# A decoder layer's last FFN: gate and up by seven half products (Strassen) for nine of eleven pairs of tiles, with the sums of weights made ahead in DRAM

## The chip, the cores and the metric

One core of one Trainium2 chip (trn2). The metric is the device time of one execution in microseconds (us). Before the change the median is 1129.5 us over 3 runs, from 1129.4 to 1129.79.

## What is computed

One layer over 512 tokens of width 1024, all in fp32: half a SwiGLU FFN with 2816 hidden columns, two token mixers side by side with one output projection, cross attention to 256 memory tokens, the same FFN again with other weights, a final norm. The part that the change touches, cut from the reference:

```python
def swiglu(h, w_gate, w_up, w_down):
    return (jax.nn.silu(h @ w_gate) * (h @ w_up)) @ w_down
...
x = x + 0.5 * swiglu(rmsnorm(x, ffn2_norm), ffn2_w_gate, ffn2_w_up, ffn2_w_down)
return rmsnorm(x, final_norm)
```

## The kernel before

Everything is held transposed: `X[d]` (d from 0 to 7) is 128 of the 1024 columns by 512 tokens. A product of two fp32 matrices is three matmuls in fp32r (`mm3`, L124 to L129): each operand is split into a high part (a copy to fp32r, made by ScalarE, ACT) and a low part (source minus high, made by VectorE, DVE), and high x high, high x low and low x high are summed in PSUM. So no weight can be used before it was loaded by a DMA that SyncE (SP) issues, copied by ACT (`whi`, L103) and subtracted by DVE (`wlo`, L104). `load_weight` (L109 to L118) does this with three pools of three buffers: raw, hi and lo. A raw buffer is free again when DVE has subtracted, a hi or lo buffer when the last matmul that reads it has ended.

The stages, in order of the trace: the first FFN (to about 460 us), the mixers (to about 560 us), the output projection `w_out` and the cross attention (to about 748 us; its eight query weights `wq` are loaded from 621 us on), the second FFN (748 to 1115 us), the last norm. `ffn` works in two chunks of 11 hidden tiles of 128 columns. For each hidden tile, gate and up are 8 x 3 matmuls each of 128x128 by 512 tokens, from one 512 KB weight each. `evacuate` (L241 to L256) multiplies the two sums by the norm's factor `R`, applies SiLU, multiplies, and splits the hidden tile. Then the down product adds the chunk's 11 tiles to each of the eight `X[d]`. The last chunk's down runs in two halves of 256 tokens (L311 to L333), with the down weights of six of the eight d kept in SBUF for the second half (tiles `wk`).

What sets the order: the framework's scheduler places the instructions when the kernel is built, for each engine apart. At run time each engine, SP's queue included, works strictly in its own order: an instruction that waits holds all behind it. In the second FFN before the change, SP's queue is weights in the order in which the matmuls need them, gate, up, gate, up, and then the down weights of the chunk.

Of the kernel before, what the change touches and what calls it, by code (L numbers as in the profile page):

```python
# [17 lines left out]
F32 = mybir.dt.float32  # L18
# [22 lines left out]
SB = 6  # L41
LINE = 512

FILL = 56

# [9 lines left out]
def body(tc, I, out):  # L55
# [3 lines left out]
    with ctx:  # L59
# [4 lines left out]
        hp = ctx.enter_context(tc.tile_pool(name="hp", bufs=40))  # L64
        wp = ctx.enter_context(tc.tile_pool(name="wp", bufs=3))
# [43 lines left out]
        def load_weight(src, shape, cuts=1):  # L109
# [8 lines left out]
            return hi, lo  # L118

# [94 lines left out]
        def ffn(norm, gate, up, down, nxt, first=None, between=None):  # L214
            h = (norm.H, norm.L)
            with tc.tile_pool(name="ffn", bufs=2) as fp:
# [40 lines left out]
                for c in range(NCHUNK):  # L257
                    hid = ([], [])
                    for j in range(CF):
                        f = c * CF + j  # L260
                        ps = []
                        for src in (gate, up):
                            if f == 0 and src is gate and first is not None:
                                w = first()
                            else:
                                w = load_weight(src[f], [KD, P])
# [4 lines left out]
                            if first is not None and f == 1 and R is None:  # L271
                                R = factor()
                        pending.append(ps)
                        if first is not None and f == 0:
                            continue
                        if R is None:
                            R = factor()
                        while pending:
                            evacuate(pending.pop(0), hid)
                    if c < NCHUNK - 1 or nxt is not None:  # L280
                        for d in range(KD):
                            w = [load_weight(down[c, d, :, j0:j1, :], [j1 - j0, P])
                                 for j0, j1 in halves]
                            down_tile(d, w, hid, slice(0, S), halves)
                            if c == NCHUNK - 1:
                                nxt.add(d)
                            elif between is not None:
                                between(d)
# [3 lines left out]
                    thirds = ((0, 4), (4, 8), (8, CF))  # L292
                    kept = {}

                    def weights(d, keep):
                        if d in kept:
                            return kept[d], thirds
                        if not keep:
                            return [load_weight(down[c, d, :, j0:j1, :], [j1 - j0, P])
                                    for j0, j1 in halves], halves  # L300
                        kept[d] = []
                        for j0, j1 in thirds:
                            raw = wp.tile([P, j1 - j0, P], F32, name="wraw3", tag="wraw")
# [591 lines left out]
```

## Time and profile before

| what | value |
|---|---|
| median of 3 runs | 1129.5 us |
| the profiled execution | 1129.09 us; its span from first to last instruction 1127.3 us |
| mean granted clock of TensorE | 0.995 |
| busy: PE / DVE / ACT / POOL | 1110.1 / 590.9 / 425.0 / 74.3 us |
| second FFN's gate, up and first down (748 to 1050 us) | PE busy 301.52 of 302 us |
| second FFN's last down, two token halves (1050 to 1115 us) | PE busy 65.00 of 65 us |
| tail after it (1115 to 1127.3 us) | PE busy 2.26 us |

PE is TensorE's matmuls, PEld its weight loads, DVE is VectorE, ACT ScalarE, POOL GpSimd, SP SyncE, which issues DMAs. A row of the groups of instructions (by line, engine and form) gives line, engine, operation, output and input tiles with shape, count, then busy us and the mean ns of one, then the idle time before them. The waits view gives total us, times, longest. A windows row gives the stretch, its length, each engine's busy us with the count of instructions, and, at its end, the granted clock, the DMA share and GB/s. A timeline row begins with start and duration in us. A profiled matmul's duration is longer than the distance to the next, since matmuls overlap in the array; what counts is start to start.

### The profile page before, as it was taken

What the parts mean: (1) busy time and instruction counts of PE and PEld (TensorE: products, weight loads), DVE (VectorE), ACT (ScalarE), POOL (GpSimd) and SP (SyncE); (2) the same over time, 40 slices, a digit from 0 to 9 for tenths busy, and PEclk for the clock granted to TensorE, in tenths of its full rate; (3) what the DMA queues carried; (4) which work ended last, traced back from release to release, by engine and by line L of the source; (5) the groups of instructions that cost most, each with busy time, mean ns of one, the idle gap of its engine ahead of it and who ended that gap; (6) DMA issues with size and microseconds to landing.
All of it is one profiled execution on the core that took longest, in us unless ns stands there. A gap on an engine that the chain in (4) does not pass through costs nothing. (4 is left out here: it accounts for less than half of the span.)

```text
span 1127.3 us, 13958 instructions
## 1 busy us (share of the span) xinstructions
PE 1110.1 (98%) x5472; PEld 934.7 (83%) x5472; DVE 590.9 (52%) x1027; ACT 425.0 (38%) x672; POOL 74.3 (7%) x98
## 2 busy tenths in 40 slices
PE   9999999999999999999989999999999999999996
PEld 7788888888888888888868988878888888888996
DVE  4544533444444447679796555455444334445542
ACT  6333312233233434568665344333332222333421
POOL 2000100000002200011121000120000000000011
PEclk9999999999999999999999999999999999999998
DMA  6322334222233423110136421222222333223511
GB/s 220 113 94 89 115 89 126 105 94 94 72 92 109 149 90 108 38 48 29 57 118 203 147 75 57 72 97 90 98 93 66 103 113 111 95 94 115 155 64 38
DMA packets 39698, 110.79 MB, mean 98 GB/s; under 512 B 4432, under 2 KB 9296, under 8 KB 39632
## 3 DMA queue, kind: packets, MB, share of 16 engines
q1 hardware_dynamic: 39632, 109.89, 30.3%
q8 instruction: 43, 0.70, 0.2%
q14 instruction: 23, 0.19, 0.1%
HBM read 107.78 MB, written 2.10 MB: 97 GB/s over the span
## 5 line engine op out<-in xcount | busy, mean ns | idle before, releaser
L103 ACT ACTIVATE whi<-wraw 128x1024 fp32r<-128x1024 f32 (+2 forms) x213 | 202.8, 953 | 513.9 <-PE acc L128 298.6
L104 DVE TENSOR_TENSOR wlo<-wraw,whi 128x1024 fp32r<-128x1024 f32 (+2 forms) x213 | 237.0, 1115 | 163.0 <-ACT whi L103 162.7
L127 PE MATMUL acc<-hH,whi 128*128 128x512 f32 x768 | 301.0, 392 | 0.6 <-ACT hH L202 0.6
L128 PE MATMUL acc<-hL,whi 128*128 128x512 f32 x768 | 299.4, 390 | 0.8 <-DVE hL L203 0.8
L129 PE MATMUL acc<-hH,wlo 128*128 128x512 f32 x768 | 299.4, 390 | 0.5 <-DVE wlo L104 0.5
L128 PEld LDWEIGHTS acc<-hL,whi 128*128 128x128 f32 x768 | 144.3, 188 | 31.5 <-DVE hL L203 1.5
L127 PEld LDWEIGHTS acc<-hH,whi 128*128 128x128 f32 x768 | 144.3, 188 | 31.4 <-ACT hH L202 1.0
L129 PEld LDWEIGHTS acc<-hH,wlo 128*128 128x128 f32 x768 | 144.3, 188 | 30.7 <-DVE wlo L104 1.0
L127 PE MATMUL acc<-hidH,whi 128*128 128x512 f32 (+1 forms) x308 | 115.6, 375 | 0.0
L129 PE MATMUL acc<-hidH,wlo 128*128 128x512 f32 (+1 forms) x308 | 115.3, 374 | 0.0
L128 PE MATMUL acc<-hidL,whi 128*128 128x512 f32 (+1 forms) x308 | 115.3, 374 | 0.0
L170 POOL TENSOR_TENSOR sq<-sq 128x512 f32<-128x512 f32 (+1 forms) x39 | 49.2, 1260 | 775.5 <-ACT sq L178 775.1
L247 DVE TENSOR_TENSOR u<-acc,R 128x512 f32<-128x512 f32 x44 | 30.4, 690 | 121.6 <-PE acc L129 121.6
L243 DVE TENSOR_TENSOR gp<-acc,R 128x512 f32<-128x512 f32 x44 | 30.4, 691 | 85.4 <-PE acc L129 81.7
L129 PEld LDWEIGHTS acc<-hidH,wlo 128*128 128x128 f32 x308 | 58.1, 189 | 10.3
L128 PEld LDWEIGHTS acc<-hidL,whi 128*128 128x128 f32 x308 | 58.1, 188 | 10.3
L127 PEld LDWEIGHTS acc<-hidH,whi 128*128 128x128 f32 x308 | 58.1, 189 | 10.2
L127 PE MATMUL acc<-whi,hH 128*128 128x512 f32 x160 | 62.5, 391 | 0.0
L129 PE MATMUL acc<-whi,hL 128*128 128x512 f32 x160 | 62.4, 390 | 0.0
L230 DVE SCALAR_TENSOR_TENSOR x<-acc,x 128x512 f32<-128x512 f32 (+1 forms) x40 | 23.3, 584 | 74.6 <-PE acc L129 74.6
L128 PE MATMUL acc<-wlo,hH 128*128 128x512 f32 x160 | 62.3, 390 | 0.0
L178 ACT ACTIVATE sq<-x 128x512 f32<-128x512 f32 (+1 forms) x48 | 26.1, 551 | 41.5 <-DVE x L230 38.9
(213 smaller groups left out, 1488.1 us busy)
## 6 DMA issues: line engine op xcount, KB each, us to landing
wraw<-up SPq DMA_DIRECT2D x44, 512.0 KB, 3.5
wraw<-gate SPq DMA_DIRECT2D x43, 512.0 KB, 3.5
wraw<-down SPq DMA_DIRECT2D x28, 384.0 KB, 3.1
wraw<-w_in SPq DMA_DIRECT2D x20, 512.0 KB, 3.5
wraw<-down SPq DMA_DIRECT2D x28, 320.0 KB, 2.9
wraw<-w_out SPq DMA_DIRECT2D x16, 256.0 KB, 2.7
wraw<-wv SPq DMA_DIRECT2D x8, 512.0 KB, 3.5
wraw<-wk SPq DMA_DIRECT2D x8, 512.0 KB, 4.2
```

The source lines that it names most:

```text
L103: ins = nc.scalar.activation(hi, src, AF.Copy)
L104: nc.vector.tensor_sub(lo, src, f32(hi))
L127: nc.tensor.matmul(ps, lhsT=aH, rhs=bH, start=start, stop=False)
L128: nc.tensor.matmul(ps, lhsT=aH, rhs=bL, start=False, stop=False)
L129: nc.tensor.matmul(ps, lhsT=aL, rhs=bH, start=False, stop=stop)
L170: nc.gpsimd.tensor_add(self.parts[0], self.parts[0], sq)
L178: nc.scalar.activation(sq, src, AF.Square)
L230: nc.vector.scalar_tensor_tensor(X[d][:, tok], acc, 0.5, X[d][:, tok], op0=ALU.mult, op1=ALU.add)
L243: nc.vector.tensor_mul(gp, ps[0], R)
L247: nc.vector.tensor_mul(u, ps[1], R)
```

## The change

The second FFN becomes a function of its own, `ffn_last`. Its 22 hidden tiles are taken as 11 pairs. The first two pairs (`PLAIN`) are done as before. For each of the other nine, gate and up (s = 0 and 1) are done by Strassen's method in Winograd's form: the weight block of two tiles by 1024 rows is cut in four quarters (two tiles, two halves of the 8 k-blocks), the token operand in four (two halves of k, two halves of the tokens), and instead of eight quarter products seven are made, each of 4 x 3 matmuls of 128x128 by 256 tokens. They run in the order 1, 5, 6, 2, 7, 3, 4.

- Four of the seven need sums of weight quarters (products 5, 6, 7, 3). `sum_step` makes them in DRAM long before: four plain copies of 256 KB issued by SP, and four accumulating DMAs of 256 KB issued by GpSimd. There are 18 such sums, nine pairs times two; ten steps run in the first FFN, eight ahead of the query weights of the cross attention, and two more flush the last accumulations.
- The token operands of the products (`operands`, four times) are built from `X`, gain and `R` by DVE and split by ACT and DVE, between the plain tiles' work. `R` goes into them, so the evacuation of the nine pairs does not multiply by it.
- The weights of products 1, 6, 7, 4 use the three-buffer pools (gate and up in one 128x1024 tile); those of 5, 2 and 3 come as two 128x512 tiles each (`wq`, with halves `wqh`, `wql`) in the big pool `hp`, which also holds the hidden tiles.
- Products are combined by adding in PSUM and by copies (ACT, `p1`, `p5`, `v`, 128x256) and adds (DVE).
- The chunks are now 4, 6, 6 and 6 tiles instead of 11 and 11, so the down product runs three times over all 512 tokens, and once, for the last 6 tiles, in two halves of 256 tokens. All eight down weights are now kept for the second half.

```diff
+PLAIN = 2
+ORDER = (1, 5, 6, 2, 7, 3, 4)
+KH = KD // 2
...
+        sums, todo = {}, [(n, j) for j in range(PLAIN, NF // 2) for n in range(2)]
+        def sum_step():
+            m = len(sums)
+            def add(i, src, back):
+                if 0 <= m - back < len(todo):
+                    n, j = todo[m - back]
+                    a = (I["gate2"], I["up2"])[n]
+                    nc.gpsimd.dma_start(sums[n, j][i], src(a[2 * j], a[2 * j + 1], sums[n, j]),
+                                        accum_op=ALU.add)
+            if m < len(todo):
+                n, j = todo[m]
+                a = (I["gate2"], I["up2"])[n]
+                a1, a2 = a[2 * j], a[2 * j + 1]
+                t = dram.tile([P, 4, KH, P], F32, name=f"sums{n}_{j}")
+                sums[n, j] = {i: t[:, x] for x, i in enumerate((5, 6, 7, 3))}
+                with tc.issue_after(last["dma"].ins):
+                    for i, src in ((5, a2[:, :KH]), (7, a2[:, :KH]), (6, a1[:, :KH]),
+                                   (3, a1[:, KH:])):
+                        nc.sync.dma_start(sums[n, j][i], src)
+            else:
+                sums[None, m] = None
+            add(5, lambda a1, a2, s: a2[:, KH:], 0)
+            add(7, lambda a1, a2, s: a1[:, :KH], 0)
+            add(6, lambda a1, a2, s: s[5], 1)
+            add(3, lambda a1, a2, s: s[6], 2)
...
+                        each(f)
...
+        LO, HI = slice(0, S // 2), slice(S // 2, S)
+        def ffn_last(norm, gate, up, down, sums):
+            h = (norm.H, norm.L)
+            with tc.tile_pool(name="spad", bufs=1) as spad, \
+                    tc.tile_pool(name="sp", bufs=1) as sp, \
+                    tc.tile_pool(name="ffn", bufs=1) as fp:
+                nc.vector.memset(spad.tile([P, SHIFT], F32, name="spad")[:, 0:1], 0.0)
+                R = None
+                B11, B2 = ([], []), ([], [])
+                T13, T24 = ([], []), ([], [])
+                def operands(k):
+                    x = []
+                    for d in (k, k + KH):
+                        t = hp.tile([P, S], F32, name="xg", tag="h")
+                        nc.vector.scalar_tensor_tensor(t, X[d], gcol(norm.off, d), R,
+                                                       op0=ALU.mult, op1=ALU.mult)
+                        x.append(t)
+                    a, b = x
+                    t13 = hp.tile([P, S], F32, name="t13", tag="h")
+                    nc.vector.tensor_sub(t13[:, LO], a[:, LO], a[:, HI])
+                    nc.vector.tensor_sub(t13[:, HI], b[:, HI], a[:, HI])
+                    t24 = hp.tile([P, S], F32, name="t24", tag="h")
+                    nc.vector.scalar_tensor_tensor(t24[:, LO], b[:, HI], -1.0, t13[:, LO],
+                                                   op0=ALU.mult, op1=ALU.subtract)
+                    nc.vector.scalar_tensor_tensor(t24[:, HI], t24[:, LO], -1.0, b[:, LO],
+                                                   op0=ALU.mult, op1=ALU.subtract)
+                    for n, pair, src in (("b11", B11, a[:, LO]), ("b2", B2, b),
+                                         ("t13", T13, t13), ("t24", T24, t24)):
+                        for i, hl in enumerate("hl"):
+                            pair[i].append(sp.tile([P, src.shape[-1]], F32R, name=f"{n}{hl}{k}"))
+                        split(pair[0][k], pair[1][k], src)
...
+                def weights_of(i, j):
+                    raws = []
+                    for n, src in enumerate((gate, up)):
+                        raws.append({1: src[2 * j][:, :KH], 2: src[2 * j][:, KH:],
+                                     4: src[2 * j + 1][:, KH:]}.get(i) if i in (1, 2, 4)
+                                    else sums[n, j][i])
+                    if ORDER.index(i) % 2:
+                        w = []
+                        for src in raws:
+                            raw = hp.tile([P, KH, P], F32, name="wq", tag="h")
+                            last["dma"] = nc.sync.dma_start(raw, src)
+                            pair = tuple(hp.tile([P, KH, P], F32R, name=n, tag="h")
+                                         for n in ("wqh", "wql"))
+                            split(*pair, raw)
+                            w.append(pair)
+                        return w
+                    raw = wp.tile([P, 2, KH, P], F32, name="wraw", tag="wraw")
+                    hi = wp.tile([P, 2, KH, P], F32R, name="whi", tag="whi")
+                    lo = wp.tile([P, 2, KH, P], F32R, name="wlo", tag="wlo")
+                    for n, src in enumerate(raws):
+                        last["dma"] = nc.sync.dma_start(raw[:, n], src)
+                    split(hi, lo, raw)
+                    return [(hi[:, n], lo[:, n]) for n in range(2)]
+                def strassen(j, hid):
+                    right = {1: (B11, LO), 2: (B2, LO), 3: (B2, HI), 4: (T24, HI),
+                             5: (T13, LO), 6: (T24, LO), 7: (T13, HI)}
+                    W = {i: weights_of(i, j) for i in ORDER}
+                    z = [acc_tile()[:, HI] for _ in range(2)]
+                    b1, b5 = [None] * 2, [None] * 2
+                    p1, v, p5 = [None] * 2, [None] * 2, [None] * 2
+                    c1 = [c_tile(n) for n in ("g1", "u1")]
+                    c2 = [c_tile(n) for n in ("g2", "u2")]
+                    def product(ps, i, s, start):
+                        b, tok = right[i]
+                        wH, wL = W[i][s]
+                        for k in range(KH):
+                            bH, bL = b[0][k][:, tok], b[1][k][:, tok]
+                            for n, (x, y) in enumerate(((wH, bH), (wH, bL), (wL, bH))):
+                                nc.tensor.matmul(ps, lhsT=x[:, k], rhs=y,
+                                                 start=start and k == 0 and n == 0,
+                                                 stop=k == KH - 1 and n == 2,
+                                                 skip_group_check=True)
+                    def copied(ps, name):
+                        t = half_tile(name)
+                        nc.scalar.activation(t, ps, AF.Copy)
+                        return t
+                    for s in range(2):
+                        product(z[s], 1, s, True)
+                        p1[s] = copied(z[s], "p1")
+                    for s in range(2):
+                        b5[s] = aux_tile()[:, HI]
+                        product(b5[s], 5, s, True)
+                        p5[s] = copied(b5[s], "p5")
+                    for s in range(2):
+                        product(z[s], 6, s, False)
+                        v[s] = copied(z[s], "v")
+                    for s in range(2):
+                        b1[s] = aux_tile()[:, HI]
+                        product(b1[s], 2, s, True)
+                        nc.vector.tensor_add(c1[s][:, LO], b1[s], p1[s])
+                    for s in range(2):
+                        product(z[s], 7, s, False)
+                        nc.vector.scalar_tensor_tensor(c2[s][:, HI], z[s], -1.0, p5[s],
+                                                       op0=ALU.mult, op1=ALU.subtract)
+                    for s in range(2):
+                        product(b5[s], 3, s, False)
+                        nc.vector.tensor_add(c1[s][:, HI], b5[s], v[s])
+                    for s in range(2):
+                        product(z[s], 4, s, False)
+                    nc.scalar.activation(c1[0], c1[0], AF.Silu)
+                    nc.scalar.activation(c2[0][:, HI], c2[0][:, HI], AF.Silu)
+                    nc.scalar.activation(c2[0][:, LO], z[0], AF.Silu, scale=-1.0)
+                    nc.vector.tensor_mul(c1[1], c1[0], c1[1])
+                    hidden(c1[1], hid)
+                    nc.vector.tensor_mul(c2[1][:, HI], c2[0][:, HI], c2[1][:, HI])
+                    nc.vector.scalar_tensor_tensor(c2[1][:, LO], z[1], -1.0, c2[0][:, LO],
+                                                   op0=ALU.mult, op1=ALU.mult)
+                    hidden(c2[1], hid)
+                chunks = ((0, PLAIN),) + tuple((j, j + 3) for j in range(PLAIN, NF // 2, 3))
+                for c, (j0, j1) in enumerate(chunks):
+                    hid = ([], [])
+                    pending = []
+                    for j in range(j0, j1):
+                        if j >= PLAIN:
+                            strassen(j, hid)
+                            continue
+                        for f in (2 * j, 2 * j + 1):
+                            ps = [plain(f, gate)]
+                            if R is not None and f > 1:
+                                operands(2 * f - 4)
+                            ps.append(plain(f, up))
+                            pending.append(ps)
+                            if f == 0:
+                                R = rows(norm.stats.column(D))
+                            if R is not None:
+                                while pending:
+                                    evacuate(pending.pop(0), hid)
+                            if f > 1:
+                                operands(2 * f - 3)
...
+                    def weights(d):
+                        if d not in kept:
+                            raw = wp.tile([P, n, P], F32, name="wraw3", tag="wraw")
+                            nc.sync.dma_start(raw, down[d, :, f0:f0 + n, :])
+                            a, b, m = (h_tile("wk").rearrange("p (j m) -> p j m", m=P)
+                                       for _ in range(3))
+                            kept[d] = [(a, b), (m[:, 0:2], m[:, 2:4])]
+                            for pair, (i0, i1) in zip(kept[d], cut):
+                                split(*pair, raw[:, i0:i1])
...
                 def queries(d):
+                    sum_step()
...
+                for _ in range(2):
+                    sum_step()
...
+        def each(f):
+            if f % 2 == 0:
+                sum_step()
...
-        ffn(n4, I["gate2"], I["up2"], I["down2"], None)
+        ffn_last(n4, I["gate2"], I["up2"], I["down2"], sums)
```

Three places show how the queues stand now. SP's queue where a chunk ends: of the kernel before, the last gate and up weights (`wraw<-gate2`, `<-up2`) and the first down weights.

```order
L116 DMA wraw_7166<-gate2 128x1024
L116 DMA wraw_7197<-up2 128x1024
L116 DMA wraw_7239<-down2 128x768
L116 DMA wraw_7245<-down2 128x640
L116 DMA wraw_7286<-down2 128x768
L116 DMA wraw_7292<-down2 128x640
```

Of the change, the last pair of the first chunk with half products (the third of its three; `wq_7715` and `wq_7721` are the weights of its product 5, `wq_7734` and `wq_7740` of product 2, `wq_7753` and `wq_7759` of product 3; `wraw_7982` to `wraw_8060` are the down weights of d = 0 to 3):

```order
L124 DMA wraw_7982<-down2 128x768
L426 DMA wq_7479<-sums0_3_746 128x512
L426 DMA wq_7485<-sums1_3_901 128x512
L124 DMA wraw_8001<-down2 128x768
L124 DMA wraw_8034<-down2 128x768
L124 DMA wraw_8060<-down2 128x768
L426 DMA wq_7715<-sums0_4_1056 128x512
L426 DMA wq_7721<-sums1_4_1648 128x512
L426 DMA wq_7734<-gate2 128x512
L426 DMA wq_7740<-up2 128x512
L426 DMA wq_7753<-sums0_4_1056 128x512
L426 DMA wq_7759<-sums1_4_1648 128x512
```

Before, the down weights came behind all of the chunk's gate and up weights; now four of the down weights stand ahead of the six `wq` loads of the pair whose hidden tiles they multiply. `wraw_8060` takes the raw buffer of `wraw_7982`, so its issue waits until DVE has made `wlo_7984`, the low part of that weight.

ACT's queue at the same place, of the change (`p5` are the copies of product 5's sums out of PSUM, `v` of the sum after product 6, whose matmuls run ahead of product 5 in this pair):

```order
L111 ACTIVATE whi_7983<-wraw_7982 128x768
L111 ACTIVATE hidH_7698<-u1_7501 128x512
L111 ACTIVATE hidH_7704<-u2_7503 128x512
L111 ACTIVATE wqh_7717<-wq_7715 128x512
L464 ACTIVATE p5_7819<-aux_7806 128x256
L111 ACTIVATE wqh_7723<-wq_7721 128x512
L464 ACTIVATE p5_7834<-aux_7821 128x256
L464 ACTIVATE v_7848<-acc_7772 128x256
```

The copy of product 5's first sum (`p5_7819`) now stands between the splits of product 5's gate weight and of its up weight. `whi_7983` waits for the end of product 6's second half, whose weight had that buffer.

ACT's queue at the end of the last pair, of the change (`hidH` are the last two hidden tiles, `wk_10044` the first down weight of the last chunk), and PE's at the same place:

```order
L490 ACTIVATE g1_9834<-g1_9834 128x512
L111 ACTIVATE hidH_10032<-u1_9835 128x512
L111 ACTIVATE hidH_10038<-u2_9837 128x512
L111 ACTIVATE wk_10044<-wraw3_10042 128x512
L111 ACTIVATE wk_10046<-wraw3_10042 128x256
```

```order
L457 MATMUL aux_9881<-b2h3_6988,wql_9822 128x256
L166 MATMUL acc_10051<-hidH_9484,wk_10044 128x256
L167 MATMUL acc_10051<-hidL_9485,wk_10044 128x256
L168 MATMUL acc_10051<-hidH_9484,wk_10045 128x256
```

In the kernel before, the same split stands ahead of other weights and hidden tiles, in time for the matmuls that read it:

```order
L103 ACTIVATE whi_8304<-wraw_8303 128x1024
L245 ACTIVATE s_8263<-gp_8261 128x512
L103 ACTIVATE wk_8420<-wraw3_8418 128x512
L103 ACTIVATE whi_8346<-wraw_8345 128x1024
L103 ACTIVATE hidH_8268<-u_8265 128x512
```

So the first down weight's split moved from before the last gate weight's to behind both of the last hidden tiles, and no other matmul stands between product 3 (`aux_9881`) and the matmul that reads it. Outside the second FFN the orders of PE, ACT and DVE are nearly those of before; SP and POOL have the sums' DMAs added.

113 lines of the change are left out of this document (74 added, 39 removed).

## The prediction, made before the changed kernel was run

> **What bounds the kernel now.** I read the page's busy times first, then the waits, then windows over the second FFN.
>
> ```profile
> PE 1110.1 (98%) x5472; PEld 934.7 (83%) x5472; DVE 590.9 (52%) x1027; ACT 425.0 (38%) x672; POOL 74.3 (7%) x98
> ```
>
> ```profile
> ACT whi L103 <- PE acc L128: 298.6, 112, 9.2
> DVE wlo L104 <- ACT whi L103: 162.7, 111, 6.9
> PEld acc L129 <- DVE wlo L104: 4.0, 4, 2.5
> ```
>
> ```profile
> 748.00:1050.00 302.00, 301.52 (x1332) 249.05 (x1331) 140.81 (x183) 93.84 (x121) 3.16 (x2) 1.00 0.32 101
> 760.00:980.00 220.00, 220.00 (x973) 181.83 (x972) 96.58 (x129) 63.20 (x78) 0.00 (x0) 1.00 0.30 96
> 1054.00:1112.00 58.00, 58.00 (x485) 57.95 (x484) 21.02 (x48) 13.71 (x26) 8.60 (x11) 1.00 0.23 73
> ```
>
> PE is busy all the time. The waits view says why: ACT waits 298.6 us in total for PE to give weight buffers back, DVE waits for ACT, and PE waits only 4.0 us for a low part. Splits run ahead of the matmuls. Matmul counts therefore set the time as long as that lead lasts. In the second FFN, matmuls of 512 columns come every 220.00/973 = 0.2261 us (760 to 980 us), of 256 columns every 58.00/485 = 0.1196 us (1054 to 1112 us).
>
> **What the change removes on PE.** A pair of tiles had 2 x 2 x 24 = 96 matmuls of 512 columns, 21.7 us. It now has 7 x 2 x 12 = 168 of 256 columns, 20.1 us: 1.6 us less, nine times, 14.5 us. The last down loses 528 - 288 = 240 of 256 columns (28.7 us) and gives 264 of 512 columns in the other chunks' downs a rise to 384 (120 x 0.2261 = 27.1 us): 1.6 us less. In sum 16.1 us. The half products save an eighth in columns but 7% in time, since a matmul of half the width costs 0.529 of the whole. In the Trainium skill, "TensorE: Matmul & The Clock Gate", section "Back-to-back issue gap", the gap of an isolated matmul is N/2.4 + 2.5 ns; by that an estimate is 109 and 216 ns, and the saving would be 21.7 us. The trace has 119.6 and 226.1, and goes into the sum.
>
> **What the change adds elsewhere.** These rows (line, operation, tiles, count, then mean ns and waits) price the new work of DVE and of ACT:
>
> ```profile
> L104 DVE TENSOR_TENSOR wlo<-wraw,whi 128x1024 fp32r<-128x1024 f32 x139 | 173.3, 1248 | 100.2 <-ACT whi L103 100.2
> L248 DVE TENSOR_TENSOR u<-s,u 128x512 f32<-128x512 f32 x44 | 30.8, 703 | 3.8 <-ACT s L245 0.5
> L104 DVE TENSOR_TENSOR hidL<-u,hidH 128x512 fp32r<-128x512 f32 x44 | 30.1, 687 | 5.7 <-ACT hidH L103 5.6
> L203 DVE SCALAR_TENSOR_TENSOR hL<-x,gains,hH 128x512 fp32r<-128x512 f32 x32 | 29.9, 952 | 5.1 <-ACT hH L202 5.1
> L104 DVE TENSOR_TENSOR wlo<-wraw,whi 128x768 fp32r<-128x768 f32 x28 | 27.5, 981 | 2.6 <-ACT whi L103 2.5
> L104 DVE TENSOR_TENSOR wk<-wraw,wk 128x512 fp32r<-128x512 f32 x12 | 8.3, 691 | 8.3 <-ACT wk L103 8.3
> L330 DVE SCALAR_TENSOR_TENSOR o<-x,gains,aux 128x256 f32<-128x256 f32 x16 | 6.4, 476 | 1.3 <-PE aux L153 1.3
> L104 DVE TENSOR_TENSOR kL<-acc,kH 128x256 fp32r<-128x256 f32 x8 | 3.3, 418 | 0.0
> ```
>
> ```profile
> L103 ACT ACTIVATE whi<-wraw 128x1024 fp32r<-128x1024 f32 x139 | 147.2, 1060 | 373.4 <-PE acc L128 183.2 <-issue 150.2 <-PE acc L129 39.3
> L103 ACT ACTIVATE hidH<-u 128x512 fp32r<-128x512 f32 x44 | 27.8, 633 | 35.2 <-DVE u L248 35.2
> L103 ACT ACTIVATE whi<-wraw 128x768 fp32r<-128x768 f32 x28 | 23.7, 847 | 71.4 <-PE acc L128 61.7 <-issue 7.7 <-DMA wraw<-down 1.7
> L103 ACT ACTIVATE wk<-wraw 128x512 fp32r<-128x512 f32 x12 | 7.6, 632 | 10.1 <-DMA wraw<-down 10.1
> L103 ACT ACTIVATE kH<-acc 128x256 fp32r<-128x256 f32 x8 | 2.9, 366 | 0.0
> ```
>
> A pair with half products asks of DVE 4 splits of 1024 (5.0), 6 of 512 (4.1), 5 plain operations on 256 columns (2.1), 3 of three operands (1.4), one multiply (0.7) and two hidden splits (1.4): 14.7 us of PE's 20.1. ACT has 4 x 1.06 + 6 x 0.63 + 8 x 0.37 + 3 x 0.63 = 12.8 us. On average both fit. Before, a pair took 4 x 1.25 + 2 x 2.8 = 10.5 of 21.7 us on DVE, and nothing in its queue had to come back to PE within the pair. Now copies and sums of one product release the PSUM and the weights of the next, and they stand in the same queues as splits that wait for PE. So I followed the new order of the queues, instruction by instruction. Three more prices:
>
> ```profile
> 1099.14 0.28 PE L129 MATMUL acc<-hidH,wk 128*128 128x256 f32 x1
> 1099.47 0.42 DVE L230 SCALAR_TENSOR_TENSOR x<-acc,x 128x256 f32<-128x256 f32 x1 [3.54 <-PE acc L129]
> ```
>
> ```profile
> 763.12 0.33 SPq L116 DMA_DIRECT2D wraw<-up  x1
> ```
>
> ```profile
> wraw<-down SPq DMA_DIRECT2D x12, 256.0 KB, 2.7
> ```
>
> From the start of the last matmul to its consumer's start are 0.33 us, so 0.21 us after its slot of 0.12; SP takes 0.33 us per issue; 256 KB land 2.7 us after the issue.
>
> *Third pair of the chunks from tile 4 and from tile 10.* Product 5's weights (`wq_7715`) stand in SP's queue behind the fourth down weight, which waits for DVE's split of the first, which waits for ACT's copy, which waits until product 6 of the same pair gives its buffer back. From product 6's end: 0.21 + 0.85 (`whi_7983`) + 0.98 (`wlo_7984`) + 0.33 (issue of the down weight) + 2.7 (landing) + 0.63 (`wqh_7717`) = 5.7 us until product 5 starts. PE has only the first down tile's 12 matmuls in between, 2.7 us: 3.0 us idle. Then `wqh_7723` stands on ACT behind `p5_7819`, the copy of product 5's first half: 0.21 + 0.37 + 0.63 = 1.2 us, and its low part 0.69 more, of which two matmuls cover 0.24: 1.65 us. Product 7 waits for `v_7848` behind `p5_7834`: 0.21 + 0.37 + 0.37 = 0.95 us. That is 5.6 us, twice: **11.2 us**. Bounds: half, if landing and issue come early; 8 us each, if the hidden tiles' splits behind (the last down tile waits for them) are late as well.
>
> *Second pair of the three chunks.* The splits of the next pair's first weights stand among those of this pair. `wqh_7468` (product 2, up) is behind `whi_7728`, which waits for the end of the next pair's product 1: 0.21 + 1.06 + 0.63 = 1.9 us against 11 matmuls, 1.3: 0.6 us. Product 7's up half waits for a copy `v`, this for an add on DVE, this for `wlo_7729`: 0.21 + 1.06 + 1.25 + 0.42 + 0.37 = 3.3 us against 13 matmuls and that wait, 2.1: 1.2 us. The low part of the next pair's first weight is 0.7 us late in the same way. 2.5 us, three times: **7.4 us**; bounds 0 and 11.
>
> *End of the last pair.* PE's next instruction behind product 3 needs `wk_10044`, which ACT makes behind both last hidden tiles: 0.21 + 0.42 (add) + 0.70 (multiply) + 2 x 0.63 (`hidH`) + 0.63 = 3.2 us, and the low part, behind two `hidL` on DVE, 0.5 more: **3.7 us** in which nothing else is there for PE. Inside that pair the copies before products 7 and 2 cost about 1.5 us (0.95 as above, and a rest): **1.5 us**; bounds 0 and 4.5.
>
> *First chunk.* The operands are 4 x (2 x 0.95 + 2 x 0.42 + 2 x 0.48 + 0.42 + 3 x 0.69) = 24.7 us of DVE, all from the third plain tile on. With four weights (5.0), two evacuations (5.5), eight down splits and eight adds (11.0) and the next pair's first splits (5) that makes 51 us, against PE's 192 matmuls, 43.4 us. Some of it was done ahead, and some can follow: I take **3 us**, between 0 and 8. The cover gone, every us of DVE there is one of PE.
>
> *The sums.* In the first FFN a step adds four issues of 0.33 us on SP and four accumulations to two tiles' 21.7 us, beside a DMA share of a third; the three raw buffers hide it. In the cross attention it is tighter:
>
> ```profile
> 621.27 26.44 SPq L116 DMA_DIRECT2D wraw<-wq  x8
> 620.00:700.00 80.00, 80.00 (x467) 70.64 (x467) 43.66 (x85) 32.89 (x64) 0.00 (x0) 1.00 0.31 98
> q1 hardware_dynamic: 39632, 109.89, 30.3%
> ```
>
> The queue moves 109.89 MB in 30.3% of 1127.3 us, 322 GB/s. Eight steps with 1 MB copied, 1 MB accumulated and a 0.5 MB weight are 20 MB, 62 us, in the 80 us of the queries. No accumulating DMA is in the trace: if it moves twice its bytes it is 87 us, 7 late. I take **0**, between 0 and 8: 20 MB is nearest to plain copies.
>
> *Sum.* -16.1 + 11.2 + 7.4 + 3.7 + 1.5 + 3 = +10.7 us on the profiled execution's 1129.1 us (span 1127.3): 1139.8. The median of the runs is 0.4 above that execution: **1140 us**. The tail after the last down (12.3 us) stays.
>
> **The rivals.** *All waits covered.* If splits keep the lead that the waits view shows today, only PE's count remains: 1129.5 - 16 = 1113 us, to 1120 with a few small waits. For it speaks the average load (14.7 and 12.8 of 20.1 us); against it the order, in which the fourth down weight cannot be issued before product 6 ends, whatever the durations are. *Half the waits*: 16.1 - 13.4, 1127 us (1120 to 1131), if landing and splits come faster than the means, as where DVE works back to back. *Slower still, through the clock.* In the output projection, where DVE is the bound today, this happens:
>
> ```profile
> 572.00:576.00 4.00, 3.35 (x15) 2.44 (x13) 4.00 (x6) 3.76 (x7) 2.21 (x1) 1.00 0.00 0
> 576.00:580.00 4.00, 0.83 (x3) 0.42 (x4) 4.00 (x7) 1.31 (x3) 1.27 (x1) 1.00 0.00 0
> 580.00:584.00 4.00, 4.00 (x11) 3.10 (x12) 4.00 (x6) 1.79 (x3) 1.99 (x2) 0.60 0.41 135
> ```
>
> PE idles 3.8 of 8 us behind DVE's queue, and in the next 4 us the granted clock is 0.60: 1.6 us lost again. The two third pairs and the end of the last pair have waits of that size (3.0 to 3.7 us): 3 to 4 such places are 6 us, and with accumulations 7 us late in the cross attention and the upper bounds of two terms (third pairs +5) it is 1158 us or more, to 1170. In the Trainium skill, "TensorE: Matmul & The Clock Gate", section "What's actually happening", about 3.4 us of idleness put the clock to half for as long; the trace agrees (0.60 over 4 us).
>
> **How the numbers follow.** My forecast (1131 to 1156) has 0.52, all covered 0.26, half 0.13, slower still 0.09. A difference under 0.2% (2.3 us, 1127.2 to 1131.8) can't be told from none. Of the half case 0.08 is faster and 0.05 the same; a hundredth of the forecast is the same too. Faster 0.34, same 0.06, slower 0.60. The range is 1113 to 1157: it leaves out most of the last case and a little of the first.
>
> **What would show it.** PE's matmul counts: 168 per pair, 0.12 us apart. The waits view should name `wqh`, `v` and `wk` copies on ACT and `wql` on DVE as what PE waits for, some 27 us in sum, most of it in the third pairs, with a gap of 3 us ahead of product 5 and one of 3.7 us ahead of the last down. In SP's queue the product 5 loads should be issued within 0.4 us of the split of the first down weight. The cross attention should take as long as before. It is wrong if PE stays at 98% or more through the half products: then the queues had more lead than I found. It is also wrong if the gaps lie elsewhere, say in the cross attention or the first chunk.

## The result, and the profile after

1187.2 us median over four runs (1183.2 to 1191.7) against 1129.6: the ratio is 1.051, with a 95% interval from 1.0466 to 1.0554. The profiled execution, the fastest of the four, took 1183.2 us; its span is 1181.4 us, 54.1 us more than before. The forecast had the sign, but not the size: 1187 lies far above its range (1113 to 1157), and above the 1170 us of the worst rival.

From the page after: busy times, the DMA queues (packets, MB, share of 16 engines' time), and issues with their time to landing.

```profile
PE 1120.7 (95%) x6000; PEld 958.3 (81%) x6000; DVE 650.1 (55%) x1163; ACT 477.1 (40%) x803; POOL 133.9 (11%) x170
...
q1 hardware_dynamic: 61520, 141.49, 38.9%
q0 software_dynamic: 10368, 18.88, 11.1%
...
sums<-gate SPq DMA_DIRECT2D x36, 256.0 KB, 6.9
sums<-sums POOLq DMA_DIRECT2D x36, 256.0 KB, 6.0
...
wq<-sums SPq DMA_DIRECT2D x36, 256.0 KB, 4.0
...
wraw<-wq SPq DMA_DIRECT2D x8, 512.0 KB, 12.9
```

The last row is the first thing to see: the cross attention's query weights landed 12.9 us after their issue (3.5 before). The waits view after, for PE, names what it waited for:

```profile
PE aux L457 <- ACT wqh L111: 15.3, 12, 2.9
PE aux L166 <- ACT qH L111: 10.2, 3, 4.7
PE acc L457 <- ACT v L464: 7.0, 10, 1.0
PE acc L168 <- DVE wlo L112: 4.0, 6, 2.1
PE acc L166 <- ACT wk L111: 3.0, 1, 3.0
```

`qH` is the cross attention. Of the `wlo` row, 2.1 us stand in the output projection, as before the change, and 1.4 us in the second FFN; the other rows are the half products and the last down. The windows view shows the two stages that lost (length, busy time of PE, PEld, DVE, ACT and POOL, granted clock, DMA share, GB/s). The first row is the cross attention's queries and scores, the others are the stretch around the third pair of the second chunk with half products.

```profile
620.00:700.00 80.00, 67.10 (x360) 57.99 (x359) 32.31 (x66) 24.84 (x46) 16.54 (x20) 0.89 1.05 246
...
1000.00:1004.00 4.00, 1.28 (x7) 0.74 (x5) 0.35 (x1) 0.63 (x1) 0.00 (x0) 1.00 0.92 319
1004.00:1008.00 4.00, 2.79 (x15) 2.10 (x14) 1.03 (x2) 0.90 (x2) 0.00 (x0) 0.68 0.42 153
1008.00:1012.00 4.00, 3.25 (x14) 2.96 (x15) 0.51 (x1) 1.69 (x4) 0.00 (x0) 0.50 0.00 0
1012.00:1016.00 4.00, 4.00 (x21) 4.00 (x21) 0.31 (x2) 0.00 (x0) 0.00 (x0) 0.54 0.00 0
```

In the cross attention the 16 DMA engines are busy all the time, and PE idles for 12.9 of 80 us (before: none, with a DMA share of 0.31). In the second FFN PE idles, and then the granted clock falls to half for some 10 us, more than the stretch of 4 us in the output projection that the forecast showed.

From start to start of matmuls on PE's timeline, less 0.2268 or 0.1197 us for the matmul's own slot, and counting gaps over 0.35 us, the 54 us come from:

| place | forecast, us | measured, us |
|---|---|---|
| cross attention: second FFN starts at 766.7 instead of 748.35 | 0 (bound 8) | 18.4 |
| matmul slots saved | -16.1 | -16 to -18 |
| first chunk | 3 | 3.6, of which 1.05 were there before |
| first and second pairs | 7.4 | 11.8 |
| third pairs of the first two chunks with half products | 11.2 (bound 16) | 7.0 + 7.6 |
| inside the last pair | 1.5 (bound 4.5) | 4.7 |
| end of the last pair | 3.7 | 3.7 |
| slower clock in the second FFN (4 us windows) | 0, in a rival 6 | 12.0 |

The slots saved follow from the run without extra weights below. The rest, 2 to 4 us, is in smaller gaps, which are not in the table.

The chain that the forecast walked through stands in the trace link by link. SP's queue and ACT's queue in the third pair of the first chunk, then the PE rows that ended the gaps there and at the last pair's end (in square brackets: idle time and releaser):

```profile
883.01 8.68 SPq L124 DMA_DIRECT2D wraw<-down  x3
891.79 0.85 SPq L426 DMA_DIRECT2D wq<-sums  x2
```

```profile
889.50 0.84 ACT L111 ACTIVATE whi<-wraw 128x768 fp32r<-128x768 f32 x1 [2.81 <-issue]
890.29 1.15 ACT L111 ACTIVATE hidH<-u 128x512 fp32r<-128x512 f32 x2
895.58 0.63 ACT L111 ACTIVATE wqh<-wq 128x512 fp32r<-128x512 f32 x1 [4.14 <-DMA wq<-sums]
899.53 0.38 ACT L464 ACTIVATE p<-aux 128x256 f32<-128x256 f32 x1 [3.32 <-PE aux L457]
899.81 0.62 ACT L111 ACTIVATE wqh<-wq 128x512 fp32r<-128x512 f32 x1
```

```profile
896.26 0.58 PE L457 MATMUL aux<-t13h,wqh 128*128 128x256 f32 x1 [2.31 <-ACT wqh L111]
...
900.48 0.39 PE L457 MATMUL aux<-t13h,wqh 128*128 128x256 f32 x1 [0.99 <-ACT wqh L111]
...
1130.43 0.39 PE L166 MATMUL acc<-hidH,wk 128*128 128x256 f32 x1 [3.02 <-ACT wk L111]
```

Three down weights are issued up to 891.7, product 5's weights at 891.79. They land at about 895.5, 3.8 us later and not 2.7. That is most of what the term for the third pairs lacked; the rest are waits of 0.6 us ahead of product 7's second half, and matmuls that come every 0.21 us at the half clock instead of 0.12.

### The profile page after: what moved, and what is told of

It is laid out like the page before. It is cut to its first block, busy times and chain, and to the rows that moved or that the text cites. A ratio compares the mean times of both kernels' runs of the same rounds, so it can differ in the third digit from the quotient of the medians.

```text
span 1181.4 us, 15710 instructions
## 1 busy us (share of the span) xinstructions
PE 1120.7 (95%) x6000; PEld 958.3 (81%) x6000; DVE 650.1 (55%) x1163; ACT 477.1 (40%) x803; POOL 133.9 (11%) x170
## 3 DMA queue, kind: packets, MB, share of 16 engines
q0 software_dynamic: 10368, 18.88, 11.1%
## 5 line engine op out<-in xcount | busy, mean ns | idle before, releaser
L111 ACT ACTIVATE whi<-wraw 128x1024 fp32r<-128x1024 f32 (+3 forms) x213 | 202.0, 950 | 425.2 <-PE acc L167 201.7
L112 DVE TENSOR_TENSOR wlo<-wraw,whi 128x1024 fp32r<-128x1024 f32 (+3 forms) x213 | 236.3, 1112 | 178.7 <-ACT whi L111 177.7
L166 PE MATMUL acc<-hH,whi 128*128 128x512 f32 x480 | 189.4, 395 | 0.0
L168 PE MATMUL acc<-hH,wlo 128*128 128x512 f32 x480 | 187.7, 391 | 0.5 <-DVE wlo L112 0.5
L167 PE MATMUL acc<-hL,whi 128*128 128x512 f32 x480 | 187.6, 391 | 0.5 <-DVE hL L242 0.5
L166 PE MATMUL acc<-hidH,whi 128*128 128x512 f32 x304 | 119.0, 392 | 2.2 <-ACT whi L111 1.7
L168 PE MATMUL acc<-hidH,wlo 128*128 128x512 f32 x304 | 118.5, 391 | 1.4 <-DVE wlo L112 1.4
L167 PE MATMUL acc<-hidL,whi 128*128 128x512 f32 x304 | 118.8, 391 | 0.0
L167 PEld LDWEIGHTS acc<-hL,whi 128*128 128x128 f32 x480 | 90.6, 189 | 19.9 <-DVE hL L242 0.9
L166 PEld LDWEIGHTS acc<-hH,whi 128*128 128x128 f32 x480 | 90.8, 189 | 19.4 <-issue 0.5
L168 PEld LDWEIGHTS acc<-hH,wlo 128*128 128x128 f32 x480 | 90.4, 188 | 19.6 <-DVE wlo L112 1.0
L166 PEld LDWEIGHTS acc<-hidH,whi 128*128 128x128 f32 x304 | 57.1, 188 | 15.0 <-ACT whi L111 2.1
L166 PE MATMUL acc<-whi,hH 128*128 128x512 f32 x160 | 62.5, 391 | 0.0
```

The source lines that it names most:

```text
L111: ins = nc.scalar.activation(hi, src, AF.Copy)
L112: nc.vector.tensor_sub(lo, src, f32(hi))
L166: nc.tensor.matmul(ps, lhsT=aH, rhs=bH, start=start, stop=False)
L167: nc.tensor.matmul(ps, lhsT=aH, rhs=bL, start=False, stop=False)
L168: nc.tensor.matmul(ps, lhsT=aL, rhs=bH, start=False, stop=stop)
```

## The experiments

### The cross attention: sums early, and sums without accumulation

Sums made in the first FFN only:

```diff
 def each(f):
-    if f % 2 == 0:
+    if f % 2 == 0 or f in (13, 17):
         sum_step()
...
 def between(d):
+    sum_step()
...
 def queries(d):
-    sum_step()
...
-for _ in range(2):
-    sum_step()
```

> All 18 sums are made in the first FFN (every second hidden tile as in the change, two more tiles, and the eight down steps of its first chunk); none is left in the cross attention. Theory A (in the cross attention the sums fill the DMA engines, so the query weights come late): the second FFN starts near 748 us as before the change instead of 767, and the time falls by some 18 us from 1187 to 1165 to 1171. Theory B (the sums cost what they cost wherever they run, the first FFN having no room either): the first FFN gets longer by 10 us or more, and the time falls by less than 8 us.

Measured: 1169.2 us, ratio to before 1.034 (1.028 to 1.039), 18 us under the change (its four runs lie between 1158.6 and 1172.6). The second FFN starts at 748.5 us. The first FFN carries all 18 sums without a loss (its DMA share rises to 0.90 up to 230 us, and PE is as busy as before). The row of the cross attention is back to what it was:

```profile
620.00:700.00 80.00, 80.00 (x467) 70.62 (x466) 43.62 (x85) 33.07 (x64) 0.00 (x0) 1.00 0.31 98
```

Theory A holds, B falls.

The accumulating DMAs left out, copies kept (the products with sums use unsummed weights):

```diff
 def add(i, src, back):
     if 0 <= m - back < len(todo):
-        nc.gpsimd.dma_start(sums[n, j][i], ..., accum_op=ALU.add)
+        pass
```

> The accumulating DMAs are left out; the plain copies stay, so products 5, 6, 7 and 3 use unsummed weights and the output is not the layer's. Theory A1 (the accumulating DMAs make the load in the cross attention): with 8 MB of copies and 4 MB of query weights in 80 us the queries are in time, the second FFN starts at 748 to 751 us, and the time falls by 16 to 19 us. Theory A2 (the copies, four issues ahead of each query weight in SP's queue, are the cost): the second FFN still starts at 758 us or later, and less than 9 us are gained.

Measured: 1166.8 us over two runs, 1.033 (1.031 to 1.035), 20 us under the change and so a little more than theory A1's 16 to 19; the second FFN starts at 749.3 us. The windows row of this run for the same 80 us:

```profile
620.00:700.00 80.00, 80.00 (x465) 70.63 (x465) 42.94 (x84) 33.94 (x64) 0.00 (x0) 1.00 0.62 200
```

With the same issues on SP ahead of each query weight PE is full. So it is the accumulations (A1) that fill the engines: 8 of 20 MB by my count, but 0.43 of a share of 1.05. Theory A2 falls.

### The chunks alone

```diff
 def sum_step():
+    return
     m = len(sums)
...
-if j >= PLAIN:
-    strassen(j, hid)
-    continue
...
-if R is not None and f > 1:
-    operands(2 * f - 4)
...
-if f > 1:
-    operands(2 * f - 3)
```

> No half products, no sums, no operands: all eleven pairs plain, with the change's chunks of 4, 6, 6 and 6 tiles and its last down in two halves. Theory A (the loss comes with half products and sums): 1128 to 1132 us, 1.6 us of matmuls less than before and a few small waits. Theory C (three more chunk boundaries and the eight kept down weights are a good part of the loss): 1140 us or more.

Measured: 1133.7 us, 1.0035 (1.0022 to 1.0047), 2 us above theory A's range. The new chunks cost 4 us instead of bringing 1.6. Of these 5.8 us, 3.4 are the gap ahead of the last down's first weight, which stands behind the last hidden tiles here as well, and 1.7 are the slower clock behind it. Theory C falls.

### Product 5's loads ahead of the down weights

```diff
-last["dma"] = nc.sync.dma_start(raw, src)
+last["wq"] = last["dma"] = nc.sync.dma_start(raw, src)
...
+def down_weight(d, f0, n):
+    if "wq" not in last:
+        return load_weight(down[d, :, f0:f0 + n, :], [n, P])
+    with tc.issue_after(last["wq"].ins):
+        return load_weight(down[d, :, f0:f0 + n, :], [n, P])
...
-w = [load_weight(down[d, :, f0:f0 + n, :], [n, P])]
+w = [down_weight(d, f0, n)]
...
```

> As the change, but the loads of a chunk's down weights are ordered behind the product 3 weights of the chunk's last pair, so product 5's loads no longer wait for a down weight. Theory A (order of SP's queue, and the clock after the long gaps): the gaps of 2.5, 2.9 and 3.1 us ahead of product 5 in the third pairs go, the granted clock stays at 1.0 there (some 10 us more), and the time falls from 1187 to 1165 to 1175. Theory D (the wait only moves: the first down weight is then late, and PE has nothing else there): within 5 us of 1187.

Measured: 1169.2 us, 1.035 (1.032 to 1.038), 18 us under the change. Gaps over 0.35 us fall from 38.5 to 28.0 us, and what the slower clock took from 12.0 to 3.4 us. The third pair of the first chunk in this run, PE's rows ahead of product 5 and ACT's:

```profile
892.34 0.39 PE L463 MATMUL aux<-t13h,wqh 128*128 128x256 f32 x1 [1.16 <-ACT wqh L111]
892.56 0.28 PE L463 MATMUL aux<-t13l,wqh 128*128 128x256 f32 x1
893.23 0.39 PE L463 MATMUL aux<-t13h,wql 128*128 128x256 f32 x1 [0.39 <-DVE wql L112]
```

```profile
890.61 1.15 ACT L111 ACTIVATE hidH<-u 128x512 fp32r<-128x512 f32 x2 [2.36 <-DVE u L499]
891.67 1.13 ACT L111 ACTIVATE wqh<-wq 128x512 fp32r<-128x512 f32 x2
```

The wait ahead of product 5's first half falls from 2.3 to 1.2 us; those on the first down weight and the one ahead of its second half are gone. The 1.2 us that are left come from ACT's order: both weights of product 5 are copied behind two hidden tiles, which wait for DVE. Theory A holds; about half of its gain is the clock.

### Both

The sums in the first FFN only, and product 5's loads ahead of the down weights, together.

> Sums all in the first FFN and product 5's loads ahead of the down weights. Theory A (the two losses lie in different stages and add up): 1187 - 18 - 18 = 1151, between 1146 and 1156 us. Theory B (they share a cause, the DMA engines, so the second remedy gains little once the first is there): 1160 us or more.

Measured: 1150.6 us, 1.018 (1.016 to 1.020): the two losses add up.

### What is left: order on ACT, or the products' own chain

With both remedies, high parts of the weights of products 5, 2 and 3 on GpSimd:

```diff
-split(*pair, raw)
+nc.gpsimd.tensor_copy(pair[0], raw)
+nc.vector.tensor_sub(pair[1], raw, f32(pair[0]))
```

> As the run with both remedies, but the high parts of the weights of products 5, 2 and 3 are made by GpSimd instead of ACT, so on ACT they no longer stand behind copies that wait for PE. Theory A (the order of ACT's queue holds what is left): the gaps ahead of products 5 and 2 (1.3, 0.9, 0.6 us in each pair) go, 8 to 12 us less than the run with both remedies, some 1140 us. Theory E (GpSimd's copy, 1.5 us by its 512-column row, is too slow or stands behind something else): within 3 us of that run, or slower.

Measured: 1143.1 us, 1.012 (1.011 to 1.014), 7.5 us less, just under theory A's 8 to 12. In the second pairs waits stay under a new name, since the load itself comes late; this is PE's row ahead of product 5 in the second pair of the last chunk:

```profile
1051.77 0.39 PE L464 MATMUL aux<-t13h,wqh 128*128 128x256 f32 x1 [1.65 <-POOL wqh L429]
```

With both remedies, no weights for products 5, 2 and 3 (they read those of 1, 6 and 7; no load, no split; all matmuls and copies stay):

```diff
-W = {i: weights_of(i, j) for i in ORDER}
+W = {i: weights_of(i, j) for i in (1, 6, 7, 4)}
+last["wq"] = last["dma"]
+W[5], W[2], W[3] = W[1], W[6], W[7]
```

> As the run with both remedies, but the weights of products 5, 2 and 3 are neither loaded nor split: these products read those of products 1, 6 and 7, so the output is not the layer's; all matmuls, copies and sums remain. Theory A (late weight splits in the queues hold PE): all gaps ahead of products 5, 2 and 3 go, and the time is 1137 us or less. Theory F (the products' own chain of copies and sums between PE, ACT and DVE holds PE, whatever the splits do): 1146 us or more.

Measured: 1118.1 us, 0.990 (0.988 to 0.992). The second FFN takes 354.1 us from first to last matmul against 366.6 before, with 6.7 us of gaps, none of them in a half product: the slots saved are 18 us by this run, 16.1 by the forecast's count (the half products' matmuls came every 0.118 us, not 0.1196). PE's two longest waits in this second FFN are for the last down's first weight and for DVE's adding of the first chunk's down sums:

```profile
PE acc L166 <- ACT wk L111: 1.8, 1, 1.8
PE acc L166 <- DVE x L390: 1.5, 1, 1.5
```

Theory F falls: the products' chain of copies and sums holds nothing once the extra weights are left out. The waits come with these weights; whether by the order of the queues or by the work itself, this run does not tell.

### The last down's first weights

Split ahead of the last hidden tiles, first with the loads ahead of the last pair's own:

```diff
+if j == NF // 2 - 1:
+    f0, n = 2 * j0, 2 * (j1 - j0)
+    last["wq0"] = last["wq"]
+    strassen(j, hid, lambda: [weights(d) for d in range(2)])
+    continue
...
+if mid is not None:
+    mid()
 for s in range(2):
     product(z[s], 4, s, False)
...
+with tc.issue_after(last["wq0"].ins):
+    nc.sync.dma_start(raw, down[d, :, f0:f0 + n, :])
...
```

> As the run with both remedies, but the first two down weights of the last chunk are loaded and split before the last pair's end, ahead of the last hidden tiles on ACT. Theory A: the gap of 3.2 + 0.55 us at the last pair's end and the slower clock behind it (1.2 us) go: 4 to 5 us less than the run with both remedies. Rival: the splits then delay the last pair's own copies, and less than 2 us are gained.

Measured: 1149.2 us, 1.017 (1.015 to 1.019): 1.4 us less, within the scatter of these runs (4.4 and 5.5 us), so the rival. The gaps at the end fall from 3.6 us to 0.4, but the down weights' loads stand ahead of the last pair's product 5 weights in SP's queue (three of them from 1061.8 to 1072.8 us, product 5's at 1072.9), and this is PE's row ahead of that product:

```profile
1078.72 0.58 PE L463 MATMUL aux<-t13h,wqh 128*128 128x256 f32 x1 [4.64 <-ACT wqh L111]
```

The same splits, with the loads behind the pair's own (`last["wq"]` is this pair's last load for product 3, `last["wq0"]` was that of the pair before), and GpSimd's copies of the high parts:

```diff
-with tc.issue_after(last["wq0"].ins):
+with tc.issue_after(last["wq"].ins):
```

> Both remedies, the high parts of the weights of products 5, 2 and 3 on GpSimd, and the first two down weights of the last chunk loaded behind this pair's own weights but split ahead of its last hidden tiles. Theory A: the 3.1 + 0.55 us at the last pair's end and 1.2 us of slower clock go without a new gap inside that pair: 1143 - 5 = 1138 us. Rival (as in the run with early down weights alone, the wait moves into the last pair): 1141 us or more.

Measured: 1135.1 us, 1.0050 (1.0033 to 1.0067), 8 us less than without the early down weights; the granted clock stays at 1.0 through the second FFN. Theory A holds, and 3 us more came off than it said: the run without them also had a wait of 2.6 us in its first pair of half products, which this one does not have; why not stays open.

### A version that beats both

The loads of products 5, 2 and 3 issued by GpSimd, six ahead of six copies. The order that put SP's down weights behind them is left out with it:

```diff
+def loads_of(j):
+    out = {}
+    for i in (5, 2, 3):
+        out[i] = []
+        for n, src in enumerate((gate, up)):
+            raw = hp.tile([P, KH, P], F32, name="wq", tag="h")
+            nc.gpsimd.dma_start(raw, src[2 * j][:, KH:] if i == 2 else sums[n, j][i])
+            out[i].append(raw)
+    return out
...
+early = loads_of(j)
...
-for src in raws:
-    raw = hp.tile([P, KH, P], F32, name="wq", tag="h")
-    last["wq"] = last["dma"] = nc.sync.dma_start(raw, src)
+for raw in early[i]:
...
```

> As that run, but the loads of products 5, 2 and 3 are issued by GpSimd, six of a pair at a time ahead of its six copies, so they no longer wait in SP's queue behind loads for which the three-buffer pool has no room. Theory A (late issue in SP's queue is what is left of the wqh gaps): the gaps ahead of product 5 (0.6 to 1.8 us in the second pairs) and the low parts in the third pairs (1.45 us) go, 5 to 10 us less: 1128 to 1133 us. Rival (DVE's order and the copies v are the rest, or GpSimd's issues cost as much as they free): 1136 us or more.

Measured: 1125.9 us, 0.9967 (0.9956 to 0.9977): 3.7 us faster than the kernel before, better than theory A's range. PE's waits in its second FFN:

```profile
PE acc L467 <- ACT whi L111: 3.2, 3, 1.1
PE acc L166 <- DVE gp L401: 2.7, 1, 2.7
PE acc L166 <- ACT whi L111: 1.7, 2, 0.9
PE acc L166 <- DVE x L390: 1.4, 1, 1.4
```

`wqh`, `wql` and `v` are not among them any more. So the last waits on copies `v`, too, came with the late weights; that they did so through DVE's sums is a reading, not shown by itself. What is left is DVE in the first chunk (`gp`, `x`), the first weight of the third pairs (`whi`, L467) and the first down weight of two chunks (`whi`, L166). In the first of these third pairs ACT starts that split at 851.42, 0.25 us after the start of the last matmul of the second pair's product 6 (851.17), which had the buffer that it needs: the pool has three, and products 7 and 4 take the other two.

The operands' low parts, three of four, on GpSimd:

```diff
-split(pair[0][k], pair[1][k], src)
+nc.scalar.activation(pair[0][k], src, AF.Copy)
+eng = nc.vector if n == "t24" else nc.gpsimd
+eng.tensor_sub(pair[1][k], src, f32(pair[0][k]))
```

> As the last run (1126), but three of the four low parts of each operand block (b11, b2, t13) are made by GpSimd instead of DVE. Theory A (in the first chunk DVE is the bound, 51 us of work against 43 of PE): 1.8 us of DVE less per block, the gaps of 2.85 and 1.5 us there and the slower clock behind them (3 us) go: 1120 to 1123 us. Rival (GpSimd, which now also issues and copies, becomes late for the first pair, or slows DVE): 1125 us or more.

Measured: 1127.6 us, 0.9981 (0.9972 to 0.9990): no gain, the rival. One group of DVE in the first chunk (775 to 815 us), of the run before and of this one:

```profile
L112 DVE TENSOR_TENSOR wlo<-wraw,whi 128x512 fp32r<-128x512 f32 x6 | 3.9, 680 | 0.0
```

```profile
L112 DVE TENSOR_TENSOR wlo<-wraw,whi 128x512 fp32r<-128x512 f32 x6 | 6.2, 1042 | 0.0
```

The mean of 1042 ns hides one long instruction. Five of the six took 0.67 to 0.68 us, as before; the sixth took 2.86 us, and all of it but the last 0.6 us lies beside two subtractions of GpSimd:

```profile
808.00 2.86 DVE L112 TENSOR_TENSOR wlo<-wraw,whi 128x512 fp32r<-128x512 f32 x1
```

```profile
807.74 1.32 POOL L372 TENSOR_TENSOR b2l<-xg,b2h 128x512 fp32r<-128x512 f32 x1
809.01 1.29 POOL L372 TENSOR_TENSOR t13l<-t,t13h 128x512 fp32r<-128x512 f32 x1
```

Over 780 to 815 us DVE runs 40 instructions instead of 54, but is busy for 31.7 of 35 us in both, since some of them take longer beside GpSimd's subtractions.

## Why the prediction was right and wrong

The five terms for waits, 26.8 us by the forecast, measured 38.5, of which 1.05 were there before. With them alone corrected the sum would be some 1151 us, inside the range. What carried the time out of it are two terms that the likeliest sum put at nothing: the sums (18.4 us) and the clock in the second FFN (12.0 us). The gaps in the cross attention are also the sign of being wrong that the prediction named last.

- **What bounds, and the slots.** PE's count is close: with weights out of the way the half products bring 18 us, not 16.1.
- **Third pairs and the last pair.** The mechanism (down weights ahead of product 5's in SP's queue) is shown: reordering alone takes 10.5 us of gaps away. The term was too small for two reasons. Landing took 3.8 to 4.0 us for these loads, not the 2.7 us of the row that I took, and in the last pair the same order holds with two down weights, which the step "Inside that pair the copies before products 7 and 2 cost about 1.5 us" passed over: product 5 waited 2.9 us there.
- **Second pairs.** 4.0, 4.0 and 3.1 us instead of 2.5; 0.7 us more in a first pair. Mechanism right: late weights and copies behind splits. Their cause, though, is the late issue in SP's queue as much as ACT's order, as GpSimd's loads show.
- **End of the last pair.** 3.7 us, as walked. The run with the chunks alone has 3.4 us of it without a half product.
- **The sums.** This is the first step that failed: "I take **0**, between 0 and 8: 20 MB is nearest to plain copies." It was 18.4 us. The accumulating queue moved 18.88 MB in 11.1% of the 16 engines' span, 144 GB/s, less than half of the 322 of plain loads. With this rate the step's own sum is 12 MB at 322 and 8 MB at 144 GB/s, 93 us in the 80 us of the queries, 13 late where the bound had 7. PE's gaps there are 14.3 us, and its matmuls at the half clock (17 us in two stretches from 647 to 685, 10.65 of them busy) took some 5 us more. The copies alone do fit, as the step said of copies.
- **The clock.** This is the other. It had its own rival, with 1.6 us a place and a chance of 0.09. It took 12 us in the second FFN, up to 5 us in one place. The step that failed is the separation: the gaps stood in the likeliest sum, and the slow clock behind them in a rival alone, though the two mostly come together. In the traces of the change and of the experiments, 19 of the 21 gaps of 2.4 us or more in the second FFN have the half clock begin in them or within 2.1 us behind them. That does not hold for every gap: the one of 2.97 us at 880 us in the run without accumulations has none, and eight stretches of half clock begin behind gaps of 0.6 to 1.8 us. How long it lasts differs as well; two windows rows of the change, the first with gaps of 1.3 and 1.0 us in it, the second behind the gap at the last pair's end:

```profile
1005.47:1015.71 10.24, 8.50 (x38) 7.69 (x37) 1.39 (x2) 2.59 (x6) 0.00 (x0) 0.50 0.02 9
1131.76:1135.17 3.41, 3.41 (x18) 3.41 (x17) 1.71 (x4) 0.58 (x3) 0.00 (x0) 0.50 0.72 220
```

In the Trainium skill, "TensorE: Matmul & The Clock Gate", section "What's actually happening", the clock returns after about 3.4 us of sustained work. The trace agrees: it was back after 3.4 us where PE worked through, and after 10.2 us where PE was still interrupted.

- **The rival "all waits covered"** fell on the order alone, as argued.
- **The spread of the change's runs** (8.5 us, against 0.7 before) goes with the clock: from the fastest to the slowest of the four, the mean granted clock was 0.978, 0.975, 0.970 and 0.969, which makes 26 to 37 us of clock lost over the span. That it comes from waits that just reach, or just miss, the clock's fall fits this, but was not tried by itself.

## What to carry to other kernels

When an algorithm saves matmuls and adds operands, read the order of every queue, and price each place where a load that is needed now stands behind a load that waits for a buffer: here 18 us, half of it through the clock, without a single instruction more. A transfer of a kind that the trace doesn't show needs a bound from its reads and writes, in the stage with the least room, and a gap of 2.4 us or more on TensorE should be priced with a slow clock behind it, as likely rather than certain (19 of 21 here, 1.7 to 6.8 us each). Before giving such a change up, run it with the extra weights left out: 1118 us said that the products themselves were worth 11 us, and moving sums, loads and splits to where there was room brought 3.7 of them.

## What was not expected of the hardware

- Accumulating DMAs of 256 KB landed 6 to 7.5 us after their issue, no later than the plain copies of the same sums (6.9 and 8.3 us), and yet taking them out lowered the DMA share in the cross attention from 1.05 to 0.62.
- GpSimd's copy of 128x512 to fp32r took 0.61 us at the least and 0.79 to 0.94 us on average (single ones up to 2.1 us), not the 1.5 us of its other operations on 512 columns, and could be used beside DVE.
- One of DVE's splits of 128x512 took 2.86 us instead of 0.68 beside two subtractions of GpSimd. In the Trainium skill, "SBUF — State Buffer", section "Who interferes with whom", a DVE instruction with two SBUF inputs contends with a GpSimd instruction that reads SBUF. The trace agrees: this split has two inputs in SBUF, and the five that ran beside no subtraction took 0.67 to 0.68 us.
